# Conv operands from chunks held in SBUF, second product pairs, prepared conv-output weights and moved places in a one-core hybrid decoder layer

## The chip, the cores and the metric

One core of a Trainium2 chip runs the whole layer. The metric is device time in microseconds (us), the median of the timed runs, lower is better. The engines are named as the profile names them: PE (matrix products), PEld (its weight loads), DVE (vector), ACT (scalar, activations and casts), POOL (GpSimd) and SP, which computes nothing and issues DMAs. Each engine takes its instructions in the order in which they stand in its own queue, so an instruction that waits holds everything behind it on that engine; a DMA issue that waits on SP or POOL holds the later issues of that queue.

## The reference

The input `x` has 2048 tokens of width 1024, float32, one layer:

```python
h = rms_norm(x, norm_g)
u = jnp.einsum('bsd,dc->bsc', h, w_in)
v_c, b_c, c_c, z_c, q, k, v, z_a, gate_logits = jnp.split(u, SPLIT_POINTS, axis=-1)
y_c = b_c * causal_depthwise_conv(c_c * v_c, conv_w)      # width 3
y_c = y_c * jax.nn.silu(z_c)
y_a = jnp.einsum('bsc,cd->bsd', y_c, w_conv_out)
q = rms_norm(q.reshape(b, s, N_Q_HEADS, HEAD_DIM), q_norm_g)    # 16 heads of 64
k = rms_norm(k.reshape(b, s, N_KV_HEADS, HEAD_DIM), k_norm_g)   # 4 heads
o = sliding_window_attention(q, k, v, sinks) * jax.nn.silu(z_a)  # window 128, sink per head
y_b = jnp.einsum('bsc,cd->bsd', o, w_attn_out)
g_a, g_b = jnp.split(jax.nn.sigmoid(gate_logits + gate_b), N_BRANCHES, axis=-1)
return x + jnp.einsum('bsd,de->bse', g_a * y_a + g_b * y_b, w_out)
```

## The kernel before

**Tiles and units.** The tokens are worked on in two tiles `t` of 1024. Everything is kept transposed, features on the partitions. A *unit* produces 256 output features for the 1024 tokens of a tile, as a 2x2 problem (two halves of 128 features, two halves of 512 tokens) with seven instead of eight products; a product is 12 matmuls of 128x512 (4 chunk pairs, and three float32r terms: high x high, high x low, low x high) in `product` (L674). The names in the profile follow: `X`, `V`, `Y` are the PSUM banks of a unit, `w..._ah/_al`, `_sh/_sl`, `_th/_tl`, `_d` its weights for products 1 and 2, 5 and 6, 3 and 7, and 4, each as a high and a low part, and `oph`, `ophc`, `ophy`, `ophwo` are the seven forms of the right-hand operand (the normalised input, the gated attention output, the gated conv output, the output weights). Forms 5, 6, 7 and 4 are made of sums and differences of raw chunks on DVE; every form is then split by `op_split` (L339): a cast on ACT for the high part and a subtraction on DVE for the low part. There are 28 buffers for forms.

`sunit` runs one unit, seven products, with some banks' values passed through the one bank `Y`. `spair` runs two units side by side, product by product (1, 1, 2, 2, 5, 5, ...), with its own banks for the second.

**Weights.** `plan` lists the units; `piece`, called once a tick, casts and splits the next weights into a ring of 8 buffers (`wpool`). For the first two units of `yb` (the attention output projection) the high and low weights of all products are made once, in tile 0 (`prepare`), written to DRAM (`wpd`) and fetched in both tiles (kind `"L"` of the plan, L516).

**What sets the order.** A *tick* is one product of PE. `put(n, f)` places a piece of work at tick `n`, and `run` emits, after each product, what stands at that tick. So the tables of numbers at the head of the file fix the order on ACT, DVE, POOL and SP; the hardware waits come from buffers and semaphores alone. Buffers are given out in rotation: `big` (19 of 128x512), `upool` (2 of 128x1026), so a tile may have to wait until the last reader of a much earlier one is done.

**The places that matter here**, in order of time:

- The next tile's statistics (`next_stats`, L1883 and L849): eight blocks of `x` are loaded into `upool` and squared on ACT at the ticks `STAT_AT`.
- Attention: 32 blocks per tile, each a row of steps at fixed distances from its tick in `STEPS_0/1`; the step with the products `po` (L1371) comes 13 ticks after the scores. Its operands go through ACT (`xh`, `yp`), DVE (`xl`) and four selections on POOL (L1354).
- `z` and `za` units (the two SiLU gates), while in tile 0 `prepare` makes the `yb` weights and the next tile is normalised, and in tile 1 `wo_sums` reads the output weights into `upool`, and writes four differences per chunk pair to DRAM (`wsd`).
- Keys of tile 1 (`fin_k`): their inverse root mean squares are turned into rows, written to DRAM (`krd`), read back spread over 64 partitions (`krb`, L1185), and DVE multiplies the keys by them (`scaled`). `K_AT` has the distances: sums, spread (2 ticks between two of four), scaled.
- The end of tile 1: `yb` of tile 1 (4 units: one pair, two single), `ya` (the conv output projection) of tile 0 and of tile 1 (4 units each: one pair, two single), then the output projection. A `ya` result is multiplied by its gate `th` (loaded from `gd` into `upool`, L1505) and added to `mt` in DRAM by a DMA of POOL with accumulation (L1520).
- The operand of `ya`: the gated conv output lies in DRAM (`ocd`). `csum` loads its chunks on SP (`cr`), makes the four sums on DVE and writes them to DRAM (`csd`); `conv_op` loads each of the 28 forms' source, a raw chunk or a sum, on POOL (`oc`) and splits it.

Of the kernel before, what the change touches and what calls it, by code (L numbers as in the profile page):

```python
# [15 lines left out]
P = 128  # L16
# [42 lines left out]
K_AT = (1, 0, 2)  # L59
V_TURN = 2  # L60
# [15 lines left out]
CSUM_0 = (2, 14, 11, 20)  # L76
CSUM_1 = (54, 66, 67, 76)
CONV_0 = (2, 3, 1, 3, 0, 7, 2, 8, 4, 0, 7, 6, 4, 11, 11, 1, 1, 8, 11, 12, 12, 16, 13, 16, 16, 12, 8, 15)
CONV_1 = (5, 0, 0, 2, 1, 2, 0, 6, 8, 5, 7, 9, 5, 11, 11, 0, 8, 8, 11, 10, 16, 15, 14, 16, 16, 11, 12, 13)
# [8 lines left out]
ROOTS_AT = (-39, -37, -17, -8)  # L88
NX_LOAD0 = (10, 9, 8, 11, 12, 8, 13, 12)
NX_LOAD1 = (15, 15, 15, 14, 18, 17, 17, 20)  # L90
NX_1 = (16, 16, 19, 18)
NX_2 = (19, 19, 22, 27)
NX_SUM5 = (20, 17, 20, 21)
NX_5 = (21, 17, 21, 22)
NX_SUM6 = (22, 22, 23, 25)
NX_6 = (24, 26, 26, 29)
NX_SUM7 = (22, 18, 21, 23)
NX_3 = (20, 29, 27, 26)
NX_SUM4 = (25, 29, 29, 33)
NX_7 = (25, 19, 29, 34)  # L100
NX_4 = (36, 30, 29, 36)
# [24 lines left out]
CA0_4 = (16, 15, 16, 16)  # L126
CA1_4 = (17, 17, 18, 18)
CA0_FIRST = (3, 3, 5, 10)
CA1_FIRST = (1, 4, 4, 10)
CA0_SECOND = (9, 9, 7, 12)  # L130
CA1_SECOND = (5, 6, 9, 11)
CA0_THIRD = (14, 13, 15, 11)
CA1_THIRD = (14, 13, 14, 11)
CA0_LAST = (13, 13, 11, 15)
CA1_LAST = (16, 14, 14, 15)
# [19 lines left out]
def block_kernel(  # L155
# [59 lines left out]
    csd = [dram.tile([4, KP, P, H], F32, name=f"csd{t}") for t in range(NT)]  # L215
# [411 lines left out]
    def piece():  # L627

        if not todo and (len(ready) > used[0] or not open_prep()):
            return None  # L630
        n, i, cost, last, f = todo[0]
        if tick[0] < held.get(n, 0):
            return None
        need = [2 * n + i] if plan[n][0] == "P" else [2 * n, 2 * n + 1][: 1 + min(i, 1)]
        if live[0] + cost > WRING or any(k not in raws for k in need):
            return None
        todo.pop(0)
        live[0] += cost
        rawlive[0] -= last
        return f()  # L640
# [495 lines left out]
    def fin_k(t):  # L1136
# [3 lines left out]
        def fin(i, q, val):  # L1140
# [20 lines left out]

            put(tick[0] + K_AT[0], sums)

# [7 lines left out]
        def turned(r):  # L1171
# [435 lines left out]
    for t in range(NT):  # L1607
# [244 lines left out]
    def attention(t, places):  # L1852
        for r, n in enumerate(places):
# [17 lines left out]
            put(n + O_, step("o", lambda g, j=j, b=b: att_values(t, j, b, g["w"], g["v"])))  # L1871
            put(n + O_ + 1, step("z", lambda g, j=j, b=b: att_out(t, j, b, g["o"])))
            put(n + S_, step("t", lambda g, j=j, b=b: att_sum(t, j, b, g["z"])))
# [73 lines left out]
    conv = [{} for _ in range(NT)]  # L1947

    def csum(t, n, j):
        raw, to = {}, csd[t]  # L1950

        def ld():
            for i in range(2):
                for q in range(2):
                    o = raw[i, q] = slot([P, H], F32, f"cr{t}_{j}_{i}_{q}")
                    nc.sync.dma_start(o, ocd[t][2 * j + i, :, hs(q)])

        def out(m, a, b, c):
            sub(a, b, c)
            nc.sync.dma_start(to[m, j], a)  # L1960

        put(n, ld)
        put(n + 2, lambda: out(0, raw[0, 0], raw[0, 1], raw[0, 0]))
        put(n + 3, lambda: out(1, raw[0, 1], raw[1, 1], raw[0, 1]))
        put(n + 4, lambda: out(2, raw[1, 1], raw[1, 1], raw[0, 0]))
        put(n + 5, lambda: out(3, raw[1, 0], raw[1, 0], raw[1, 1]))

    def conv_op(t, n, m, j):
        src = {8: (0, 1), 1: (0, 0), 2: (1, 0), 3: (1, 1)}.get(m)
        got = slot([P, H], F32, f"oc{t}_{m}_{j}")  # L1970
        if src:
            nc.gpsimd.dma_start(got, ocd[t][2 * j + src[0], :, hs(src[1])])  # L1972
        else:
            nc.gpsimd.dma_start(got, csd[t][(5, 7, 6, 4).index(m), j])
        put(n, lambda: op_split(f"y{t}", m, j, got, conv[t]))

    tick0 = 0
    for t in range(NT):
# [7 lines left out]

        attention(t, [t0 + n for n in (STEPS_0, STEPS_1)[t]])
# [143 lines left out]
```

## Time and profile before

| | |
|---|---|
| median of 3 runs | 1920.59 us (1916.62 to 1921.56) |
| the profiled execution, its own time | 1915.99 us |
| its span in the trace | 1914.3 us |
| PE busy | 1884.9 us (98%), 8622 matmuls |
| DVE / ACT / POOL busy | 1578.9 / 1004.1 / 606.1 us (82 / 52 / 32%) |
| DMA | 422.14 MB, mean 221 GB/s |
| tile 0: keys, values to `za` / `yb` | 0 to 731 us / 731 to 810 us |
| tile 1: keys, values to `za` / `yb` | 810 to 1523 us / 1523 to 1599 us |
| `ya` of both tiles / output projection | 1599 to 1756 us / 1756 to 1914 us |

PE is busy nearly throughout, so its rows are read for what is missing: where a matmul starts late, the trace gives the idle time before it and the engine whose semaphore ended it. A wait row reads "who waited <- for what: total us, times, longest us". SPq rows are DMA issues; the time beside them is that of issuing.

### The profile page before, as it was taken

Reading aid. Unit: us, or ns where it says so; the run is one execution under the profiler, and the core shown is the slowest. Engines: PE = TensorE matmul, PEld = TensorE weight load, DVE = VectorE, ACT = ScalarE, POOL = GpSimd, SP = SyncE. Lnnn points to the kernel's source line nnn. Section 1 sums busy time; section 2 is a strip of 40 time slices with the busy share of each in tenths; the row PEclk is TensorE's granted clock in tenths of the full one; section 3 lists DMA queues with packets and bytes.
Section 4 is the critical chain, followed back from the end, with each engine's and each line's share of the span. In section 5 each row is a group of like instructions: output and inputs, shape, how many; then the busy total and the mean of one; then the engine's idle time right before and its main releaser. Section 6 shows DMA issues by size and latency. Waiting matters only on the chain.

```text
span 1914.3 us, 27564 instructions
## 1 busy us (share of the span) xinstructions
PE 1884.9 (98%) x8622; PEld 1564.2 (82%) x8622; DVE 1578.9 (82%) x2643; ACT 1004.1 (52%) x1995; POOL 606.1 (32%) x874
## 2 busy tenths in 40 slices
PE   9999999999999999998999999999999999999999
PEld 7888888888887887887888888888878888778787
DVE  7988898798888878978988889888878779687654
ACT  7665455556666444455545555666643435344321
POOL 2073334335655000026424344454620012331000
PEclk9999999999999999999999999999999999999999
DMA  8286556668787789638655555787889679998653
GB/s 295 79 236 175 168 169 179 213 205 250 234 245 237 262 295 307 230 111 227 163 163 158 161 161 186 237 245 227 254 282 324 236 273 330 298 250 245 226 175 110
DMA packets 230817, 422.14 MB, mean 221 GB/s; under 512 B 30928, under 2 KB 105680, under 8 KB 220688
## 3 DMA queue, kind: packets, MB, share of 16 engines
q1 hardware_dynamic: 195456, 329.88, 52.7%
q0 software_dynamic: 32768, 86.28, 16.7%
q10 hardware_dynamic: 2448, 4.23, 0.7%
q8 instruction: 69, 1.13, 0.2%
q14 instruction: 76, 0.62, 0.1%
HBM read 282.63 MB, written 137.64 MB: 220 GB/s over the span
## 4 chain that ended last, share of the span: by engine, by line
PE 76%; DVE 7%; DMA 7%; issue 5%; ACT 3%; POOL 2%; SPq 1%; DVEq 0%; ACTq 0%; POOLq 0%
PE Y L674 29%; PE Xcv L674 3%; PE Vcv L674 3%; PE Xza L674 2%; PE Vza L674 2%; PE Vyb L674 2%; PE Xgb L674 2%; PE Vgb L674 2%; PE Xyb L674 2%; PE po L1371 2%; PE Vga L674 2%; PE Xga L674 2%; PE Vo L674 2%; PE Vb L674 2%; PE Xb L674 2%
## 5 line engine op out<-in xcount | busy, mean ns | idle before, releaser
L1333 POOL DMA_DIRECT2D x<-fd x256 | 139.9, 552 | 126.0 <-DMA fd<-f 55.7
L1306 ACT ACTIVATE p<-s,st,rq 128x128 f32<-128x128 f32 x256 | 113.0, 450 | 0.2 <-issue 0.2
L1354 POOL TENSOR_SCALAR_AFFINE_SELECT xh<-xh 64x512 fp32r<-64x512 f32 x64 | 59.8, 934 | 160.3 <-DVE xl L308 87.4
L1326 POOL DMA_DIRECT2D fd<-f x64 | 36.7, 573 | 215.5 <-DVE f L308 186.0
L1210 POOL DMA_DIRECT2D vd<-v x16 | 9.9, 622 | 220.1 <-DVE v L308 219.9
L674 PE MATMUL Xcv<-oph,wcv_ah 128*128 128x512 f32 x256 | 79.0, 390 | 0.0
L1354 POOL TENSOR_SCALAR_AFFINE_SELECT xl<-xl 64x512 fp32r<-64x512 f32 x64 | 65.7, 1027 | 4.4
L1520 POOL DMA_DIRECT2D mt<-th x32 | 27.8, 868 | 121.7 <-DVE th L308 117.7
L1972 POOL DMA_DIRECT2D oc<-ocd x24 | 14.6, 654 | 146.1 <-ACT ophc L339 119.5
L1354 POOL TENSOR_SCALAR_AFFINE_SELECT yp<-xl 64x512 fp32r<-64x512 f32 x64 | 58.5, 915 | 3.1
L1354 POOL TENSOR_SCALAR_AFFINE_SELECT yp<-yp 64x512 fp32r<-64x512 f32 x64 | 57.5, 898 | 4.2
L308 DVE SCALAR_TENSOR_TENSOR y<-u,cols,y 128x512 f32<-128x512 f32 x64 | 53.3, 833 | 3.8 <-ACT y L1420 2.7
L674 PEld LDWEIGHTS Xcv<-oph,wcv_ah 128*128 128x128 f32 x256 | 47.6, 188 | 9.6
L308 DVE TENSOR_TENSOR o<-po,o 64x256 f32<-64x256 f32 x128 | 53.4, 417 | 1.0
L308 DVE TENSOR_TENSOR p<-p,st 128x512 f32<-128x512 f32 x64 | 50.4, 787 | 3.7 <-DVE st L308 0.4
L1109 POOL DMA_DIRECT2D q2d<-q_h x64 | 44.2, 691 | 25.9 <-ACT q_h L1104 14.8
L495 ACT CAST wcv_sh<-wcv_raw 128x1024 fp32r<-128x1024 f32 x16 | 16.8, 1052 | 67.8 <-DVE wcv_raw L308 67.7
L1306 ACT ACTIVATION_READ_ACCUMULATOR p<-s,st,rq 128x1 f32 x256 | 50.5, 197 | 0.0
L674 PE MATMUL Xcv<-oph,wcv_al 128*128 128x512 f32 x128 | 49.8, 389 | 0.0
L674 PE MATMUL Y<-oph,wcv_d 128*128 128x512 f32 x192 | 46.9, 393 | 1.7 <-DVE vr L308 1.5
L1383 ACT COPY o<-po 64x256 f32<-64x256 f32 x128 | 47.1, 368 | 2.3
L1109 POOL DMA_DIRECT2D q2d<-q_l x64 | 44.1, 689 | 13.0 <-DVE q_l L308 5.2
(691 smaller groups left out, 6557.2 us busy)
## 6 DMA issues: line engine op xcount, KB each, us to landing
gd<-th SPq DMA_DIRECT2D x64, 256.0 KB, 2.7
wcv_raw<-in_w_units SPq DMA_DIRECT2D x16, 1024.0 KB, 5.5
q<-q2d SPq DMA_DIRECT2D x64, 256.0 KB, 5.5
v<-vd SPq DMA_DIRECT2D x128, 128.0 KB, 3.5
fd<-f POOLq DMA_DIRECT2D x64, 256.0 KB, 4.1
x<-fd POOLq DMA_DIRECT2D x256, 64.0 KB, 3.2
th<-gd SPq DMA_DIRECT2D x64, 256.0 KB, 5.2
x<-in_x SPq DMA_DIRECT2D x16, 512.0 KB, 6.4
```

The source lines that it names most:

```text
L308: r = f(*args, **kw)
L495: return (lambda: nc.scalar.copy(hi, src), lambda: vec.tensor_tensor(out=lo, in0=src, in1=hi.bitcast(F32), op=ALU.subtract))
L674: nc.tensor.matmul(ps, lhsT=w[:, j, :], rhs=b[:, m, :], start=start and j == 0 and i == 0, stop=j == KP - 1 and i == 2, skip_group_check=n ...
L1109: nc.gpsimd.dma_start(q2d[t][j][half, q * 2 * HB : (q + 1) * 2 * HB, i, e, :], src[HALVES[e]].bitcast(F32).rearrange("p (b x) -> p b x", x ...
L1306: nc.scalar.activation(out=p[:, i, :], in_=sg[:, i, HD : 3 * HD], func=AF.Exp, bias=st[:, 1, i : i + 1], scale=rv[:, i // 2, i % 2 : i % 2 ...
L1326: nc.gpsimd.dma_start(fd, f)
L1333: nc.gpsimd.dma_start(x[QUADS[k]], src[k])
L1354: nc.gpsimd.affine_select(out=d4, in_=s4, pattern=[[0, 2], [-32 * sg, 2], [0, G], [-sg, 32]], compare_op=ALU.is_gt if prev else ALU.is_ge, ...
L1371: nc.tensor.matmul(po[:, cs], lhsT=v2[:, kind, :], rhs=xx[:, :, h * HD : (h + 1) * HD], start=n == 0, stop=n == 2)
L1383: nc.scalar.copy(ov, pov[oth, :, e])
L1520: nc.gpsimd.dma_start(to, m, accum_op=ALU.add)
L1972: nc.gpsimd.dma_start(got, ocd[t][2 * j + src[0], :, hs(src[1])])
```

## The change

1. **Conv operand.** `csum`, `conv_op` and the DRAM tensor `csd` go. The 16 raw chunks of a tile are loaded once each, on POOL, into `big` buffers, and the sums are made in place, as the forms of the next tile's input already are (`first_sum`, `second_sum`, `third`, `last_sum`, `form`).
2. **Pairs.** In tile 1 the third and fourth `yb` units become a pair; so do the third and fourth `ya` units of tile 0. For `ya` of tile 1 they stay single.
3. **`ya` weights.** Those of the first two `ya` units are made by `prepare` in tile 1's `z`/`za` units, written to DRAM and fetched for both tiles. Two prepared pieces may be fetched in one tick.
4. **`wo_sums`** moves from tile 1's `z`/`za` units to the last gate units (two of four) and the last `za` units.
5. **Keys.** The four spreads and multiplications get ticks of their own, the value turns come one tick later.
6. **Places.** `STAT_AT` goes from 3 to 7 ticks apart; three attention blocks of tile 0 (10, 11 and 30) get their `po` products and what follows one tick later; `HOLD`, `PREP_*`, `NX_*`, `CA*`, `WO_FORM_AT` get new numbers.

```diff
-K_AT = (1, 0, 2)
-V_TURN = 2
+K_SUMS_AT = 1
+K_SPREAD = (1, 1, 5, 7)
+K_SCALED = (5, 7, 9, 11)
+V_TURN = 3
...
-CSUM_0 = (2, 14, 11, 20)
-CSUM_1 = (54, 66, 67, 76)
...
-WO_SUMS_AT = (1, 9, 18, 27)
...
+CO0_LOAD0 = (-5, -5, -9, -7, -4, -3, -3, 4)
...
+CO1_LOAD0 = (-7, -3, -2, -2, -3, -4, -3, -1)
...
+WO_SUMS_AT = (160, 169, 219, 227)
 WO_AHEAD = 3
-THS_AT = (9, 8)
-YB_PAIRS = (2, 1)
-HOLD = (9, 11, 7, 11, 9, 8, 9)
-STAT_AT = (105, 112, 116, 119, 121, 122, 125, 128)
+THS_AT = (8, 6)
+YB_PAIRS = (2, 2)
+YA_PAIRS = (2, 1)
+HOLD = (7, 11, 7, 9, 8, 7, 8, 10, 5)
+STAT_AT = (112, 119, 126, 133, 140, 147, 154, 161)
...
+VALUES_LATER = ((0, 10), (0, 11), (0, 30))
...
+PREP_E = (9, 12, 16, 16, 18, 23, 25, 30, 33, 33)
+PREP_F = (17, 25, 24, 19, 29, 32, 40, 35, 37, 35)
...
-    def piece():
+    def piece(more=True):
...
-        return f()
+        got = f()
+        if more and plan[n][0] == "L" and todo and plan[todo[0][0]][0] == "L":
+            piece(False)
+        return got
...
-                put(tick[0] + K_AT[1] + 2 * n, lambda i=i, q=q: spread(i, q))
-                put(tick[0] + K_AT[2] + 2 * n, lambda i=i, q=q: scaled(i, q))
+                put(tick[0] + K_SPREAD[n], lambda i=i, q=q: spread(i, q))
+                put(tick[0] + K_SCALED[n], lambda i=i, q=q: scaled(i, q))
...
-            paired.add(len(plan))
             for j in range(NJ):
+                if j in (0, 2)[: YA_PAIRS[i]]:
+                    paired.add(len(plan))
                 at_(("ya", i, j))
+                if j < 2:
+                    plan[-1] = ("L",) + plan[-1][1:]
...
-            put(n + O_, step("o", lambda g, j=j, b=b: att_values(t, j, b, g["w"], g["v"])))
+            late = int((t, r) in VALUES_LATER)
+            put(n + late + O_, step("o", lambda g, j=j, b=b: att_values(t, j, b, g["w"], g["v"])))
...
-    def csum(t, n, j):
...
-    def conv_op(t, n, m, j):
...
+    conv = [{"raw": {}, "ops": {}} for _ in range(NT)]
+
+    def conv_ops(t, n1):
+        st = conv[t]
+
+        def ld(c, q):
+            h = st["raw"][c, q] = slot([P, H], F32, f"oc{t}_{c}_{q}")
+            nc.gpsimd.dma_start(h, ocd[t][c, :, hs(q)])
+
+        for q, ns in enumerate(((CO0_LOAD0, CO1_LOAD0)[t], (CO0_LOAD1, CO1_LOAD1)[t])):
+            for c, n in enumerate(ns):
+                put(n1 + n, lambda c=c, q=q: ld(c, q))
...
+        for j in range(KP):
+            put(n1 + (CO0_SUM5, CO1_SUM5)[t][j], lambda j=j: first_sum(j, st))
+            put(n1 + (CO0_5, CO1_5)[t][j], lambda j=j: form(f"y{t}", 5, j, st))
...
+        if t + 1 == NT:
+            for j in range(KP):
+                wo_sums(t0 + WO_SUMS_AT[j], j)
...
-        if t == 0:
-            for j in range(2):
-                prepare(("yb", j), tick[0], (PREP_A, PREP_B)[j])
+        for j in range(2):
+            prepare((("yb", "ya")[t], j), tick[0], (PREP_A, PREP_B, PREP_E, PREP_F)[2 * t + j])
...
-                rest += y_units(i, 0, conv[i], 1)
+                conv_ops(i, n0 + 7 * (NJ * i + NJ - 2))
+                rest += y_units(i, 0, conv[i]["ops"], YA_PAIRS[i])
```

Three places where the tables move instructions. The rows are the program's order on one engine, with no time in them; line numbers of the changed kernel are larger by about 30.

ACT in tile 0, around the last conv unit and the unit `b_3`: `ACTIVATE x_` is the square of a loaded block of `x`, `COPY Y` the copy for which PE's next product waits, `CAST wb_3_..` the weights of the unit. Before:

```order
L849 ACTIVATE x_4_3779,ss_651<-x_4_3779 128x1024
L495 CAST wb_3_ah<-wb_3_raw 128x1024
L1383 COPY o_1_2_3863<-po_1_2_3821 64x4x2x32 x2
L1340 CAST xh_1_3_3866<-x_1_3_3702 128x512
L1341 CAST yp_1_3_3868<-x_1_3_3702 64x512
L849 ACTIVATE x_5_3798,ss_651<-x_5_3798 128x1024
L1402 COPY u_7_3781<-Xcv_7_3782 128x512
L495 CAST wb_3_d<-wb_3_raw 128x512
L495 CAST wb_3_sh<-wb_3_raw 128x1024
L849 ACTIVATE x_6_3898,ss_651<-x_6_3898 128x1024
```

and in the change:

```order
L522 CAST wb_3_ah<-wb_3_raw 128x1024
L1370 CAST xh_1_3_3850<-x_1_3_3694 128x512
L1371 CAST yp_1_3_3852<-x_1_3_3694 64x512
L1432 COPY u_7_3771<-Xcv_7_3772 128x512
L522 CAST wb_3_d<-wb_3_raw 128x512
L1413 COPY o_1_2_3873<-po_1_2_3843 64x4x2x32 x2
L522 CAST wb_3_sh<-wb_3_raw 128x1024
L522 CAST wb_3_th<-wb_3_raw 128x1024
L1370 CAST xh_1_4_3946<-x_1_4_3812 128x512
L1371 CAST yp_1_4_3948<-x_1_4_3812 64x512
L879 ACTIVATE x_2_3907,ss_649<-x_2_3907 128x1024
L722 COPY Y<-Xb_3_3966 128x512
```

Three squares stood among the ten rows; now there is one, ahead of the copy of `Y`, and the copy `o_1_2` of a block with later `po` now follows `wb_3_d`.

DVE in tile 1, the second and third query units: `k_.._t<-k_.._t,krb` are the key multiplications, `k_.._l` the low parts after a cast of ACT, `Vq` and `q_.._t` the sums for which PE waits. Before:

```order
L308 SCALAR_TENSOR_TENSOR q_0_1_0_l<-q_0_1_0_t,gqk,q_0_1_0_h 128x512
L308 TENSOR_TENSOR k_0_0_t<-k_0_0_t,krb_0_0_8660 128x512
L308 TENSOR_TENSOR wq_1_tl<-wq_1_raw,wq_1_th 128x1024
L308 STREAM_TRANSPOSE ptq_0_0_0_8717<-q_0_0_0_t 128x512
L308 TENSOR_TENSOR k_0_0_l<-k_0_0_t,k_0_0_h 128x512
L308 TENSOR_TENSOR k_0_0_t<-k_0_0_t,krb_0_1_8697 128x512
L308 STREAM_TRANSPOSE ptq_0_1_1_8747<-q_0_1_1_t 128x512
L308 TENSOR_REDUCE qss_0_8492<-ptq_0_0_0_8717 128x16
L308 TENSOR_TENSOR Vq_1_8728<-s5q_1_8741,Y 128x512
```

and in the change:

```order
L335 SCALAR_TENSOR_TENSOR q_0_1_0_l<-q_0_1_0_t,gqk,q_0_1_0_h 128x512
L335 TENSOR_TENSOR wq_1_tl<-wq_1_raw,wq_1_th 128x1024
L335 STREAM_TRANSPOSE ptq_0_0_0_8714<-q_0_0_0_t 128x512
L335 TENSOR_TENSOR k_0_0_t<-k_0_0_t,krb_0_0_8628 128x512
L335 STREAM_TRANSPOSE ptq_0_1_1_8736<-q_0_1_1_t 128x512
L335 TENSOR_REDUCE qss_0_8475<-ptq_0_0_0_8714 128x16
L335 TENSOR_TENSOR Vq_1_8717<-s5q_1_8730,Y 128x512
```

The first key multiplication now stands behind two instructions that do not need it, and of the other key work ahead of `Vq` nothing is left.

SP at the change from `yb` to `ya` of tile 0: `wya_.._ah/_al/_sh/_sl` are the fetched weights, `th_0_0<-gd` the first gate of the pair (into one of the two `upool` buffers), `mt<-th` results of the last `yb` units. Before, the weights came raw, 1 MB each, among the loads and stores of the sums; in the change:

```order
L1548 DMA mt_114<-th_2_1_15551 128x512 x2
L543 DMA wya_0_ah<-wpd_ya_0_13816 128x1024
L543 DMA wya_0_al<-wpd_ya_0_13816 128x1024
L1548 DMA mt_114<-th_2_2_15652 128x512
L1535 DMA th_0_0_15786<-gd_0_115 128x512 x2
L1548 DMA mt_114<-th_2_2_15652 128x512
L543 DMA wya_1_ah<-wpd_ya_0_13820 128x1024
L543 DMA wya_1_al<-wpd_ya_0_13820 128x1024
L1548 DMA mt_114<-th_2_3_15678 128x512
L543 DMA wya_0_sh<-wpd_ya_1_13817 128x1024
L543 DMA wya_0_sl<-wpd_ya_1_13817 128x1024
```

The second unit's first weights stand behind the load of `th_0_0`, which needs a buffer that the stores of `th_2_1` release. At the start of `ya` of tile 1 the order is the same, but there the buffer is released by POOL's accumulating DMAs.

More of the change, by code (lines that the diff above doesn't have):

```diff
@@ new lines @@
+CO0_SUM5 = (5, 4, 3, 6)
+CO0_SUM6 = (9, 10, 13, 14)
+CO0_SUM7 = (5, 6, 12, 12)
+CO0_SUM4 = (14, 15, 16, 21)
+CO0_1 = (0, 3, 3, 5)
+CO0_2 = (5, 6, 10, 16)
+CO0_5 = (8, 6, 5, 14)
+CO0_6 = (10, 12, 15, 19)
+CO0_3 = (8, 17, 13, 8)
+CO0_7 = (7, 8, 12, 21)
+CO0_4 = (23, 17, 16, 25)
+CO1_LOAD0 = (-7, -3, -2, -2, -3, -4, -3, -1)
+CO1_LOAD1 = (-7, -4, -2, 0, 3, 0, 0, 0)
+CO1_SUM5 = (4, 3, 5, 6)
+CO1_SUM6 = (9, 6, 12, 14)
+CO1_SUM7 = (5, 8, 8, 12)
+CO1_SUM4 = (12, 15, 14, 22)
+CO1_1 = (2, 3, 3, 2)
+CO1_2 = (5, 6, 8, 13)
@@ L1160, in reduce @@
                     put(tick[0] + 1, rms)
-            put(tick[0] + K_AT[0], sums)
+            put(tick[0] + K_SUMS_AT, sums)
         left = [4]
@@ L2019, in block_kernel @@
             next_tile(t + 1, tick[0] + 7 * 2 * NJ)
-        if t + 1 == NT:
-            for j in range(KP):
-                wo_sums(tick[0] + WO_SUMS_AT[j], j)
-        if t == 0:
-            for j in range(2):
-                prepare(("yb", j), tick[0], (PREP_A, PREP_B)[j])
+        for j in range(2):
+            prepare((("yb", "ya")[t], j), tick[0], (PREP_A, PREP_B, PREP_E, PREP_F)[2 * t + j])
         for n, (key, j, fin, _) in enumerate(zs):
-            if n == NJ - 1 and t + 1 == NT:
-                for i in range(NT):
-                    for j in range(NJ):
-                        csum(i, tick[0] + (CSUM_0, CSUM_1)[i][j], j)
             if n + 1 < len(zs):
```

118 lines of the change are left out of this document (53 added, 65 removed).

## The prediction

> **What bounds the kernel now.** First the page's head and its engine row:
>
> ```profile
> span 1914.3 us, 27564 instructions
> PE 1884.9 (98%) x8622; PEld 1564.2 (82%) x8622; DVE 1578.9 (82%) x2643; ACT 1004.1 (52%) x1995; POOL 606.1 (32%) x874
> ```
>
> PE computes nearly all the time, and the change alters none of its matmuls. What can be won or lost is PE's idle time: 1914.3 - 1884.9 = 29.4 us, plus any time at a lower clock. So the second view is that of PE's waits, longest first, over the whole span:
>
> ```profile
> PE Y L674 <- ACT Y L692: 4.0, 3, 3.2
> PE Y L674 <- DVE q_t L308: 3.1, 1, 3.1
> PE Y L674 <- DVE s5ya L308: 2.7, 1, 2.7
> PE Y L674 <- DVE Vq L308: 2.1, 2, 1.5
> PE po L1371 <- POOL xl L1354: 1.8, 2, 1.4
> PE Y L674 <- DVE vr L308: 1.5, 2, 1.2
> ...
> PE po L1371 <- POOL yp L1354: 1.3, 1, 1.3
> ...
> PE Xyb L674 <- DMA wyb_ah<-wpd_yb: 1.0, 1, 1.0
> PE Xyb L674 <- DMA wyb_al<-wpd_yb: 0.9, 2, 0.5
> ...
> PE Y L674 <- DVE Vya L308: 0.6, 1, 0.6
> ```
>
> There is no standing bottleneck behind PE, only some ten separate stalls of 1 to 3 us, each with its own cause a step or two further back. I followed each back in the timelines of ACT, DVE and POOL, and count them one by one. The sum is made against the profiled execution, 1915.99 us; the median of the runs shown, 1920.59, lies 4.6 us above it, and I add that at the end.
>
> **Term 1, the statistics (`STAT_AT`).**
>
> ```profile
> 361.56 1.06 ACT L849 ACTIVATE x<-x 128x1024 f32<-128x1024 f32 x1 [3.78 <-DMA x<-in_x]
> 380.95 1.06 ACT L849 ACTIVATE x<-x 128x1024 f32<-128x1024 f32 x1 [3.82 <-DMA x<-in_x]
> SPq L1883 <- ACT x L849: 11.5, 4, 5.7
> 384.68 1.66 PE L674 MATMUL Y<-oph,wcv_d 128*128 128x512 f32 x6 [1.22 <-DVE vr L308]
> ```
>
> The loads of `x` wait on SP for a buffer that ACT's squares release (11.5 us in four waits), so twice the square waits 3.8 us for its load, and ACT's casts behind it are late. That delays `wb_d`, then `vr` on DVE, then PE (1.22), and in the same stretch the POOL selections of `po` (the 1.4 of the `xl` row). With 7 ticks between two blocks, no load meets an unread buffer. Gain 1.4 + 1.2 = 2.6 at most. The squares now stand directly ahead of a copy of `Y` eight times, two ticks after their load; a load that is late by a microsecond there costs part of that. I take -2.4; bounds -2.6 and +0.5.
>
> **Term 2, three later `po` (`VALUES_LATER`).** Block 30 is the stall in `z`:
>
> ```profile
> 615.67 0.38 PE L1371 MATMUL po<-yp,v 128*128 128x256 f32 x1 [1.31 <-POOL yp L1354]
> 616.50 0.38 PE L1371 MATMUL po<-xl,v 128*128 128x256 f32 x1 [0.44 <-POOL xl L1354]
> 617.28 1.05 PE L674 MATMUL Y<-oph,wz_sh 128*128 128x512 f32 x2
> ...
> 620.48 0.40 PE L674 MATMUL Y<-oph,wz_sl 128*128 128x512 f32 x1
> 620.71 0.62 PE L674 MATMUL Y<-oph,wz_sh 128*128 128x512 f32 x2
> 615.00:620.00 5.00, 3.89 (x12) 3.11 (x13) 3.19 (x6) 3.70 (x7) 1.37 (x2) 0.68 1.06 345
> 890.00:895.00 5.00, 3.70 (x16) 3.06 (x17) 4.93 (x9) 3.04 (x6) 4.39 (x7) 1.00 0.91 239
> ```
>
> POOL is late by 1.31 + 0.44. The granted clock in these 5 us is 0.68 (the column before the DMA share), and the eight matmuls from 617.28 to 620.48 take 3.20 us, where at 0.23 apiece (the last step) they would take 1.84: another 1.36. The later tick, at least one product, covers the delay, so gain 1.31 + 0.44 + 1.36 = 3.1. A loss of clock does not follow every stall: at 890 to 895, with 3.07 us idle (the row at 891.30 below), the clock stayed 1.00, so I price none for new stalls. Bounds -3.1 and 0 (the delay repeats a tick later). I take -3.1. What is late next is that block's output, which no unit reads until `za`.
>
> The Trainium skill, TensorE: Matmul & The Clock Gate (What's actually happening), says that the clock falls to half after an idle window of about 3.4 us in a window that runs freely. By that rule the 1.75 us here would not lower it and the 3.07 us at 891 might; the trace shows the opposite of both. If it held for stalls above 3.4 us, the four stalls of the slower rival below would cost some 1.4 more each, 1936 for 1931.
>
> **Term 3, the key roots.**
>
> ```profile
> 875.71 0.69 DVE L308 TENSOR_TENSOR k_t<-k_t,krb 128x512 f32<-128x512 f32 x1 [3.39 <-DMA krb<-krd]
> 879.35 0.69 DVE L308 TENSOR_TENSOR k_l<-k_t,k_h 128x512 fp32r<-128x512 f32 x1 [1.17 <-ACT k_h L339]
> 884.24 0.69 DVE L308 TENSOR_TENSOR k_l<-k_t,k_h 128x512 fp32r<-128x512 f32 x1 [1.18 <-ACT k_h L339]
> 888.15 0.69 DVE L308 TENSOR_TENSOR k_t<-k_t,krb 128x512 f32<-128x512 f32 x1 [0.82 <-DMA krb<-krd]
> 891.30 1.89 PE L674 MATMUL Y<-oph,wq_d 128*128 128x512 f32 x7 [3.07 <-DVE q_t L308]
> ```
>
> DVE loses 3.39 + 1.17 + 1.18 + 0.82 = 6.6 us in waits of the key work, and `Vq` and `q_t` behind it are late: PE waits 2.1 + 3.1 = 5.2. In the new order two instructions (a low part and a transpose) move ahead of the first multiplication, and each `k_l` gets other work between itself and its cast. The first DMA wait will not go entirely: the two instructions fill about 1.9 of 3.39. With some 5 of 6.6 us recovered on DVE, both PE stalls nearly vanish; the 0.6 that the second `Vq` wait adds (2.1 - 1.5) may stay, as two multiplications move into that unit. I take -4.5; bounds -5.2 and -2. `kd` comes three ticks later, some 20 ticks ahead of the first attention load.
>
> **Term 4, `wo_sums` out of `z`, `prepare` into it.**
>
> ```profile
> 1390.24 0.60 ACT L1477 ACTIVATE zs<-Y 128x512 f32<-128x512 f32 x1 [6.92 <-DMA ocd<-zin]
> 1367.85 1.60 SPq L1576 DMA_DIRECT2D wos<-in_w_out  x2
> SPq L1469 <- DMA od<-o: 6.8, 1, 6.8
> ```
>
> PE's 3.2 on `ACT Y` is the end of this chain: SP waits 6.8 us for a buffer that `od<-o` still reads, `ocd<-zin` behind it goes late, and ACT waits for the buffer that this frees. The 1 MB of `wos` in front of `od<-o` made it slow. It leaves; but nine ticks into `z` 1 MB of `wp_ya` stands in the same position ahead of another `od<-o` and `zin`. So the stall can come back one unit later. I take -3.2 + 2.0 = -1.2; bounds -3.2 and +1.5. `prepare` itself adds 14 casts on ACT and 22 subtractions and sums on DVE, of 0.6 to 0.7 us each (the ACT row here, the DVE rows of term 3); they lie in the idle time of both engines in `za`, and where that is gone each costs PE its length.
>
> **Term 5, `csum` gone.**
>
> ```profile
> 1644.47 0.69 DVE L308 TENSOR_TENSOR cr<-cr,cr 128x512 f32<-128x512 f32 x1 [5.37 <-DMA cr<-ocd]
> 1672.95 1.04 ACT L495 CAST wya_ah<-wya_raw 128x1024 fp32r<-128x1024 f32 x1 [6.22 <-DMA wya_raw<-in_w_units]
> 1600.00:1740.00 140.00, 136.49 (x599) 111.74 (x598) 110.40 (x159) 58.26 (x86) 42.23 (x61) 1.00 0.97 281
> ```
>
> The two stalls of `ya` (0.6 on `Vya`, 2.7 on `s5ya`) come from DVE waiting for a sum's chunks and from a raw weight that lands late in a stage with a DMA share of 0.97. PE's idle time there is 140 - 136.49 = 3.5. The new order has no `cr` load, and that unit is in a pair. I take -3.5; bounds -3.5 and 0.
>
> **Term 6, raw chunks and second pairs.** Sixteen chunks sit in 19 rotating buffers, and the forms are made from them during the second `yb` pair and the second `ya` pair of tile 0. The nearest row is the second `yb` pair of tile 0 with the next tile's forms, built alike:
>
> ```profile
> 780.00:835.00 55.00, 54.41 (x239) 43.89 (x239) 53.05 (x82) 30.18 (x51) 2.47 (x4) 1.00 0.38 124
> ```
>
> PE idles 0.59 there. Two such places give +1.2. The DMA share there is only 0.38, so the upper bound is +4; the lower 0.
>
> **Term 7, fetched `ya` weights.** Two new starts with weights that need ring buffers of the pair before:
>
> ```profile
> wyb_al<-wpd_yb SPq DMA_DIRECT2D x2, 512.0 KB, 8.1
> 1522.71 10.90 PE Xyb L674 x48
> SPq L1505 <- DMA mt<-th: 55.2, 14, 9.9
> mt<-th POOLq DMA_DIRECT2D x28, 256.0 KB, 5.8
> ```
>
> At tile 0's `yb` the fetch took 8.1 us to land and PE waited 1.9; at tile 1's (1522.71) it waited 0. A product takes 10.90/4 = 2.7 us, and in a pair the second unit's first weights find a free buffer only when product 7 is done, three to four products (8 to 11 us) ahead of use. They also stand behind the load of a gate `th`, which waits for `mt<-th` to land, up to 9.9 us. So +2 at each start, +4 in all; bounds 0 and +10. In bytes little changes: at 256 KB a transfer the 64 of `csum` (16 MB), 24 of 56 `oc` (6) and four raw weights (4) go, two raw loads and 28 stores of `prepare` (9) and 56 halves of fetches (14) come, 3 MB net of some 420.
>
> The Trainium skill, DMA: Bandwidth & Descriptors (Issuing engines are not separate DMA queues), says that DMAs from all engines share the same 16 DMA engines. By it, chunk loads on POOL don't relieve the fetches on SP, which land as slowly as at 0.97; that would put term 7 near +5 rather than +4.
>
> **Sum.** -2.4 - 3.1 - 4.5 - 1.2 - 3.5 + 1.2 + 4 = -9.5: 1906.5 for a profiled execution, 1911.1 for a median. `HOLD`, `NX_*`, `CA*`, `WO_FORM_AT` and the startup I leave at nothing.
>
> **The rivals.**
>
> *All gains, no new stalls:* terms 1 to 5 at their best, 6 and 7 at 0: -2.6 - 3.1 - 5.2 - 3.2 - 3.5 = -17.6, median 1903. For it: tile 1's `yb` start without a stall. Against: PE would then idle about 13 us in the whole span.
>
> *The end gives it back:* terms 1 to 3 hold (-10), term 4 returns in full (0), and fetches and chunks cost +10 against -3.5. About -3.5, median 1917, within 0.3%. It is also what remains if the moved ticks don't remove the waits they aim at.
>
> *Slower, by SP's queue in `ya`:* the second unit's first and third weights, in both fetched `ya` pairs, stand behind a `th` load. If each of these four issues waits the 9.9 us seen, less than the lead of 8 to 11 us is left for a landing of 8.1, and PE waits 5 to 8 at each, 20 to 32 in all; with the other terms at -13.5 that is +6.5 to +18.5, median about 1931. It decides from a mean wait of 3.4 us at each of the four. For it: the 55.2 us of such waits, and POOL's queue, where chunk loads that wait for buffers stand ahead of `mt<-th`. Against: tile 1's `yb`, with stores of SP in POOL's place, shows none.
>
> **How the numbers follow.** Forecast 0.42, all gains 0.20, given back 0.18, slower 0.20. A measurement of this kernel can tell about 0.3% (5.8 us) from no change, so faster 0.62, same 0.18, slower 0.20. The likeliest case alone spans 1906 to 1916 (term 7 from 0 to +9); the range 1899 to 1930 reaches into both outer cases.
>
> **What would show it.** Right: no `x<-in_x` wait on ACT between 340 and 400; `po` at 615 without idle time and clock 1.00; DVE's `krb` wait under 2 us; PE waits of 1 to 3 us for `wya_ah`/`wya_al` at the two pair starts. Wrong: a PE wait on `wya_th` or `wya_tl`, or on `ophy` behind an `oc` load, above 3 us; ACT's `zs` again behind `ocd<-zin`; or a new wait of the gate units behind the squares.

## The result, and the profile after

The changed kernel takes 1915.55 us (median of 20 executions, 1912.27 to 1927.6), the kernel before 1919.22 us on the same chip (median of 20, 1916.35 to 1925.25): a ratio of 0.9982, with 95% between 0.9971 and 0.9993. A second set of runs gave 0.9979 (0.9970 to 0.9988). So the change gains 3.5 to 4 us where 9.5 were forecast, a fifth of a per cent: real, but under the 0.3% that the prediction drew as the line to "no change". In the table further down, an effect "against the change" is the difference to the mean of these two ratios, 0.99805, times 1919 us; each such difference is uncertain by some 3 us, one against the kernel before by some 2.

The first profile of the change comes from its slowest execution, 1927.6 us, so a second profile was taken as well, of an execution of 1913.3 us (span 1911.6). The page's head and the engine row of the first profile:

```profile
span 1925.8 us, 27444 instructions
PE 1894.3 (98%) x8622; PEld 1569.9 (82%) x8622; DVE 1568.2 (81%) x2633; ACT 996.2 (52%) x1993; POOL 593.4 (31%) x850
```

PE's idle time is 31.5 us where it was 29.4, and PE's busy time rose by 9.4 us although it computes the same 8622 matmuls: most of that is a lower clock. The view of PE's waits (engine, line, what it waited for: us in total, times, longest), same profile:

```profile
PE Y L704 <- ACT Y L722: 7.0, 5, 3.4
PE Y L704 <- DVE Vq L335: 3.2, 1, 3.2
PE Xya L704 <- DMA wya_ah<-wpd_ya: 3.0, 1, 3.0
PE Y L704 <- DVE zs L335: 2.0, 1, 2.0
...
PE Vya L704 <- DMA wya_th<-wpd_ya: 1.9, 1, 1.9
...
PE Vya L704 <- DMA wya_tl<-wpd_ya: 0.9, 2, 0.6
...
PE Xya L704 <- DMA wya_al<-wpd_ya: 0.7, 2, 0.5
PE Y L704 <- DVE q_t L335: 0.6, 1, 0.6
```

Of the rows shown of before, `s5ya` is gone, `vr` is down to 0.3, the longest of `po` fell from 1.4 to 0.7 and `q_t` from 3.1 to 0.6. `Vq` rose from 1.5 to 3.2 at its longest and `zs` from 0.6 to 2.0. New are the four rows of fetched `ya` weights (6.5 us), and a longest wait on `ACT Y` that now lies in the gate stage, at 459. So many of the stalls moved rather than vanished. What `ya` costs shows in how many matmuls run between 1600 and 1740 us, the number in brackets behind PE's busy time. Before it was 599 (the row stands in the prediction). The change, first profile:

```profile
1600.00:1740.00 140.00, 133.14 (x555) 107.23 (x554) 83.52 (x126) 41.40 (x68) 29.59 (x40) 0.95 0.87 246
```

and the second profile of the change:

```profile
1600.00:1740.00 140.00, 133.68 (x572) 108.61 (x571) 87.33 (x129) 43.20 (x69) 32.99 (x44) 0.98 0.88 248
```

At 0.227 us a matmul, 44 and 27 fewer are 10.0 and 6.1 us lost in a stage where the prediction's terms 5 to 7 come to +1.7. The DMA share there fell from 0.97 to 0.87, which speaks against a want of DMA engines as the cause of the late weights. SP's timeline of the change (start, length, line, transfer), first profile, shows what they wait for:

```profile
1611.00 0.32 SPq L543 DMA_DIRECT2D wya_th<-wpd_ya  x1
1611.41 1.40 SPq L543 DMA_DIRECT2D wya_tl<-wpd_ya  x1
1621.50 0.80 SPq L1535 DMA_DIRECT2D th<-gd  x2
1622.40 0.38 SPq L543 DMA_DIRECT2D wya_th<-wpd_ya  x1
...
1672.14 0.56 SPq L543 DMA_DIRECT2D wya_ah<-wpd_ya  x1
1672.80 0.39 SPq L543 DMA_DIRECT2D wya_al<-wpd_ya  x1
1684.01 0.85 SPq L1535 DMA_DIRECT2D th<-gd  x2
1684.96 0.38 SPq L543 DMA_DIRECT2D wya_ah<-wpd_ya  x1
```

Between 1612.8 and 1621.5, and between 1673.2 and 1684.0, SP issues nothing: it stands at a `th` load whose buffer an accumulate `mt<-th` still reads. The second unit's weights are issued right behind, and land too late. PE's timeline behind the first of the two (the bracket is the idle time before the row and its releaser):

```profile
1629.41 0.70 PE L704 MATMUL Vya<-ophy,wya_th 128*128 128x512 f32 x2 [1.87 <-DMA wya_th<-wpd_ya]
1630.69 0.79 PE L704 MATMUL Vya<-ophy,wya_tl 128*128 128x512 f32 x1 [0.58 <-DMA wya_tl<-wpd_ya]
1631.29 1.05 PE L704 MATMUL Vya<-ophy,wya_th 128*128 128x512 f32 x2
1632.14 0.63 PE L704 MATMUL Vya<-ophy,wya_tl 128*128 128x512 f32 x1
1632.57 1.05 PE L704 MATMUL Vya<-ophy,wya_th 128*128 128x512 f32 x2
```

Three matmuls take 1.28 us here (1631.29 to 1632.57), 0.427 apiece where 0.227 is usual, and the granted clock between 1630 and 1635 is 0.50. It stays so until 1636.4.

### The profile page after: what moved, and what is told of

Same layout as the page of the kernel before. It is cut to its first block, busy times and chain, and to the rows that moved or that the text cites. A ratio compares the mean times of both kernels' runs of the same rounds, so it can differ in the third digit from the quotient of the medians.

```text
span 1925.8 us, 27444 instructions
## 1 busy us (share of the span) xinstructions
PE 1894.3 (98%) x8622; PEld 1569.9 (82%) x8622; DVE 1568.2 (81%) x2633; ACT 996.2 (52%) x1993; POOL 593.4 (31%) x850
## 4 chain that ended last, share of the span: by engine, by line
PE 74%; DMA 9%; DVE 7%; issue 5%; ACT 2%; POOL 1%; SPq 1%; DVEq 0%; POOLq 0%; ACTq 0%
PE Y L704 29%; PE Vcv L704 4%; PE Xcv L704 4%; PE Xza L704 2%; PE Vo L704 2%; PE Xo L704 2%; PE Vza L704 2%; PE Vga L704 2%; PE Xgb L704 2%; PE Vb L704 2%; PE Xga L704 2%; PE po L1401 2%; PE Vq L704 2%; PE Xb L704 2%; PE Vgb L704 2%
## 5 line engine op out<-in xcount | busy, mean ns | idle before, releaser
L1988 POOL DMA_DIRECT2D oc<-ocd x32 | 19.7, 673 | 138.7 <-DMA wyb_al<-wpd_yb 116.5
L335 DVE TENSOR_TENSOR ophy<-oc,ophy 128x512 fp32r<-128x512 f32 x56 | 36.8, 685 | 23.6 <-ACT ophy L366 23.6
L366 ACT CAST ophy<-oc 128x512 fp32r<-128x512 f32 x56 | 31.8, 619 | 33.1 <-DVE oc L335 23.8
```

Of the source, the lines that this page charges most:

```text
L335: r = f(*args, **kw)
L366: nc.scalar.copy(hi, src)
L1988: nc.gpsimd.dma_start(h, ocd[t][c, :, hs(q)])
```

## The experiments

Twelve kernels ran, the change itself once more among them, each in 5 to 12 executions beside the kernel before. First the measured effects in one table.

| run | edit | ratio to before (95%) | effect, us |
|---|---|---|---|
| the change again | none | 0.9979 (0.9970 to 0.9988) | -4.0 against before |
| e1 | `th` loads of `ya` later | 0.9942 (0.9928 to 0.9956) | -7.4 against the change |
| e2 | `STAT_AT` undone | 0.9985 (0.9973 to 0.9997) | +0.9 against the change |
| e3 | `STAT_AT`, `VALUES_LATER`, keys undone | 1.0009 (0.9998 to 1.0021) | +1.7 against before, +5.5 against the change |
| e4 | squares two ticks later | 0.9960 (0.9945 to 0.9974) | -3.9 against the change |
| e5 | e1 and e4 | 0.9933 (0.9919 to 0.9948) | -9.1 against the change |
| e6 | keys undone | 1.0005 (0.9993 to 1.0018) | +4.7 against the change |
| e7 | e5, key products a tick later | 0.9938 (0.9919 to 0.9957) | -8.2 against the change |
| e8 | before with `wo_sums` moved alone | 0.9996 (0.9987 to 1.0005) | -0.8 against before |
| e9 | `VALUES_LATER` undone | 1.0010 (0.9995 to 1.0025) | +5.7 against the change |
| e10 | `ya` weights from raw loads | 0.9981 (0.9967 to 0.9995) | +0.1 against the change |
| e12 | before with the `th` loads later | 0.9986 (0.9976 to 0.9995) | -2.7 against before |

**e1, the `th` loads of `ya` behind the weights.** In the change, with the third and fourth load of a pair at ticks 8 and 9, and the next unit's first two ticks later:

```diff
-  ((0, 0), (1, 1), (outs[0][0] + 1, 2), (THS_AT[t], 3)), outs[1][0] + 1))
+  ((0, 0), (1, 1), (outs[0][0] + 1, 2), (THS_AT[t], 3)) if w
+      else ((0, 0), (1, 1), (8, 2), (9, 3)), outs[1][0] + (1 if w else 3)))
```

> The changed kernel, with the third and fourth load of th in each pair of ya, and the first for the next unit, issued some ticks later, so that on SP they stand behind the weights of the second unit and not ahead. Theory A (SP's order): in the changed kernel's profile SP waits 8.6 us (1612.9 to 1621.5) and 10.7 us (to 1684.0) at a th load for mt<-th, and wya_th and wya_ah, wya_al issued behind it are late; PE's stalls of 2.0, 0.8, 3.1 and 0.9 us for these weights (6.8 us) fall under 1 us together and the low clock behind them goes too (some 3 us more), so about 7 to 10 us faster than the changed kernel. Theory B (the fetches are late because their buffers come free late and the DMA engines are busy): the weights' issues move forward by little, the stalls stay within 1 us of 6.8, and the time stays within 2 us.

Measured: 1908.03 us, 7.4 less than the change. SP's timeline of e1:

```profile
1602.91 0.32 SPq L543 DMA_DIRECT2D wya_th<-wpd_ya  x1
1603.33 0.38 SPq L543 DMA_DIRECT2D wya_tl<-wpd_ya  x1
1605.66 0.32 SPq L543 DMA_DIRECT2D wya_th<-wpd_ya  x1
1606.07 0.38 SPq L543 DMA_DIRECT2D wya_tl<-wpd_ya  x1
1614.97 0.92 SPq L1535 DMA_DIRECT2D th<-gd  x2
```

SP still waits (1606.5 to 1615.0), but now the second unit's `wya_th` goes out 2.8 us behind the first's instead of 11.4. In the same stretch of e1:

```profile
1600.00:1740.00 140.00, 138.35 (x609) 113.93 (x608) 92.24 (x137) 47.74 (x76) 32.99 (x44) 1.00 0.93 265
```

609 matmuls instead of 555 and 572, at clock 1.00. Theory A holds; the DMA engines move more in the same time (265 GB/s for 246), so theory B falls. What stays of the fetches is PE waits of 0.5, 0.5 and 1.3 us, 2.3 together: more than the 1 us that theory A expected, and less than the +4 that the prediction gave them.

**e12, the same edit in the kernel before.**

> The kernel before with the th loads of the ya pairs later, and nothing else. The prediction's fifth term took the late raw weight and the late chunks of a sum in ya (PE's stalls of 0.6 and 2.7 us) to come from csum's transfers at a DMA share of 0.97: then 0 to 1 us, with the stalls still there. Theory A' (there too SP stood still: its th loads wait up to 9.9 us for mt<-th, with cr<-ocd and the raw weight issued right behind): 3 to 5 us faster than the kernel before, so that csum itself cost little.

Measured: 2.7 us faster than the kernel before, with `csum` still in place. In the first of these two fences is e12's stretch of `ya`, in the second its one wait of PE there:

```profile
1600.00:1740.00 140.00, 138.68 (x609) 113.69 (x609) 112.72 (x163) 59.04 (x88) 42.17 (x61) 1.00 0.98 287
```

```profile
PE Y L674 <- DVE s5ya L308: 1.3, 1, 1.3
```

The stalls of 0.6 and 2.7 us shrink to 1.3, and the matmuls rise from 599 to 609, at a DMA share of 0.98. So in the kernel before, too, most of the loss in `ya` came from the standing `th` loads, with `cr<-ocd` and the raw weight behind them, not from the amount that `csum` moved. The gain is just short of the 3 to 5 that were expected.

**e10, `ya` weights from raw loads.** No `prepare` for `ya` and no fetched halves; `HOLD` as the raw pairs had it.

```diff
-        for j in range(2):
+        for j in range(2 if t == 0 else 0):
             prepare((("yb", "ya")[t], j)
...
                 at_(("ya", i, j))
-                if j < 2:
+                if j < 0:
                     plan[-1] = ("L",) + plan[-1][1:]
...
-HOLD = (7, 11, 7, 9, 8, 7, 8, 10, 5)
+HOLD = (7, 11, 7, 9, 8, 9, 8, 8, 5)
```

> The changed kernel with the weights of the two first ya pairs formed from raw loads as before (no fetched halves of ya, none prepared in the stage of z). The prediction's seventh term: 4 us faster than the changed kernel. Theory A (behind SP's order the fetches cost 10): 7 to 10 us faster, as with the th loads moved. Rival (the conversions of four more raw units cost DVE and ACT in ya what the fetches cost SP): within 2 us of the changed kernel, with PE's waits for weights behind DVE in their place.

Measured: no difference. The waits of PE in `ya` are of other kinds, in e10's profile:

```profile
PE Xya L704 <- DVE ophy L335: 4.8, 1, 4.8
PE Vya L704 <- DVE wya_sl L335: 1.4, 1, 1.4
```

DVE's timeline ahead of the first of them has the form (`ophy`) behind four sums of raw weights and a low part, without a gap:

```profile
1610.61 2.74 DVE L335 TENSOR_TENSOR wya_raw<-wya_raw 128x512 f32<-128x512 f32 x4
1613.27 1.22 DVE L335 TENSOR_TENSOR wya_sl<-wya_raw,wya_sh 128x1024 fp32r<-128x1024 f32 x1
1614.40 0.68 DVE L335 TENSOR_TENSOR ophy<-oc,ophy 128x512 fp32r<-128x512 f32 x1
```

The rival holds: formed from raw loads, the pairs cost DVE about what the fetches cost through SP's order. e1 lies 7.5 us below e10, but e10 has the early `th` loads; raw weights with the late ones were not run, so it isn't shown that fetched weights are the better kind.

**e2 and e4, the statistics.** In e2 `STAT_AT` has its old ticks:

```diff
-STAT_AT = (112, 119, 126, 133, 140, 147, 154, 161)
+STAT_AT = (105, 112, 116, 119, 121, 122, 125, 128)
```

In e4 each square stands four ticks behind its load:

```diff
-            put(n0 + n + 2, lambda b=b: square(b))
+            put(n0 + n + 4, lambda b=b: square(b))
```

> The changed kernel with the loads of x for the next tile's statistics at their old ticks. The prediction's first term (the new places gain 2.4): about 2.4 us slower than the changed kernel. Theory A (in the gate stage the square in front of the copy of Y waits 6.3 us for its load, which SP issues behind attention's loads, and PE's stalls of 3.6 and 1.3 us, with two of 0.6, cost more than the 2.6 removed, before any loss of clock): 3 to 5 us faster than the changed kernel, with PE's waits for Y between 455 and 510 under 1 us in all.

> The changed kernel with each of the eight squares four ticks behind its load of x instead of two, so that it no longer stands in front of the copy of Y. Theory A (what costs is that the copy of Y stands behind a square that waits for its load): PE's stalls of 3.6, 1.3, 0.6 and 0.6 us on ACT's Y in the gate stage fall under 1 us together, and the time falls by 4 to 6 us with the low clock behind the first. Rival (ACT has no room for a square anywhere in the gate stage, the wait or its 1.1 us only meets the next conversion): 0 to 2 us, with new waits of PE for weights or for po.

ACT's timeline of the change (first profile) shows what the new places cost:

```profile
457.91 1.06 ACT L879 ACTIVATE x<-x 128x1024 f32<-128x1024 f32 x1 [6.32 <-DMA x<-in_x]
458.88 0.19 ACT L879 ACTIVATION_READ_ACCUMULATOR x<-x 128x1 f32 x1
458.97 0.58 ACT L722 COPY Y<-Xga 128x512 f32<-128x512 f32 x1
```

The square waits 6.3 us for its block, the copy of `Y` stands behind it, and PE waits 3.4. With the old places (e2) PE waits elsewhere:

```profile
PE Y L704 <- DVE vr L335: 3.4, 2, 3.0
```

So the term as it stands is worth 0.9 us, neither the 2.4 of the prediction nor a loss of 3 to 5. In e4 the whole rest of `ACT Y` is:

```profile
PE Y L704 <- ACT Y L722: 1.5, 2, 1.3
```

and the longest of it lies at 1382, in `z`, not in the gate stage. The gain of 3.9 us is just short of the 4 to 6 that were expected, within its uncertainty. Against the old places the later squares gain 3.9 + 0.9 = 4.8 us: the new places are worth at least the prediction's 2.4, and the wait in front of the copy ate most of it.

**e3, e6 and e9, parts of the first tile undone.** e3 undoes the three edits of terms 1 to 3, e6 the key roots, e9 the later `po`:

```diff
-VALUES_LATER = ((0, 10), (0, 11), (0, 30))
+VALUES_LATER = ()
```

```diff
-K_SPREAD = (1, 1, 5, 7)
-K_SCALED = (5, 7, 9, 11)
-V_TURN = 3
+K_SPREAD = (0, 2, 4, 6)
+K_SCALED = (2, 4, 6, 8)
+V_TURN = 2
```

> The changed kernel with the statistics, the three later po and the key roots at their old places: only the part behind them (wo_sums, prepare, the raw chunks, the second pairs and the fetched ya weights) is new. The prediction (terms 4 to 7: -1.2 - 3.5 + 1.2 + 4): 0.5 us slower than the kernel before, so about 4 us slower than the changed one. Theory A (the first three terms held at about -10 and the end costs 6 to 7): 6 to 7 us slower than the kernel before. Theory C (the first three terms gained little, since their stalls came back elsewhere, and the end is about even): 0 to 1 us faster than the kernel before, 2 to 4 slower than the changed one.

> The changed kernel with the key roots' old places. The prediction's third term: 4.5 us slower than the changed kernel. Theory D (DVE is full in the queries' stage, 9.6 of 10 us from 880 on, so that the key work only moves PE's wait from q_t, 3.1, to Vq of the next unit, 3.1): within 1.5 us of the changed kernel, with the old two stalls of about 1.4 and 3.3 us in place of 0.7 and 3.3.

> The changed kernel without the three later po. The prediction's second term: 3.1 us slower than the changed kernel, with PE's stalls of 1.3 and 0.5 us at 615 back. Rival (the gain is given back 11 us later, where PE waits 1.1 to 2.2 us for wz_d behind DVE's zs in all profiles of the change, and not before it): within 1 us of the changed kernel.

e6 lost 4.7 us, close to the prediction's term and against theory D; its waits at that place are these two:

```profile
PE Y L704 <- DVE q_t L335: 3.4, 1, 3.4
...
PE Y L704 <- DVE Vq L335: 1.6, 1, 1.6
```

They are 5.0 us for 3.8 in the change (0.6 and 3.2), so the visible waits explain 1.2 us of the 4.7 and theory D had the picture right; the rest is within the uncertainty or in the clock behind the second long stall, and stays open. e9 lost 5.7, with these rows back:

```profile
PE po L1401 <- POOL yp L1384: 2.1, 2, 1.3
...
PE po L1401 <- POOL xl L1384: 1.4, 3, 0.5
```

The prediction's 3.1 lies inside that. Its rival, that `zs` at 627 gives the gain back, falls. e3 puts the three terms together at 5.5 us, less than the 11.3 that e2, e6 and e9 add up to. With some 3 us on each, the runs don't say how much of this is an interaction.

**e8, `wo_sums` alone.** In the kernel before, `wo_sums` is issued at the change's ticks, and nothing else is changed:

```diff
-WO_SUMS_AT = (1, 9, 18, 27)
+WO_SUMS_AT = (160, 169, 219, 227)
...
+        if t + 1 == NT:
+            for j in range(KP):
+                wo_sums(t0 + WO_SUMS_AT[j], j)
         attention(t, [t0 + n for n in (STEPS_0, STEPS_1)[t]])
...
-        if t + 1 == NT:
-            for j in range(KP):
-                wo_sums(tick[0] + WO_SUMS_AT[j], j)
```

> The kernel before with one part of the change alone: the sums for wo moved out of the stage of z, to the new ticks in the attention and z stages; no prepare for ya. The prediction's fourth term at its best: SP no longer holds od<-o back, ACT's zs don't wait 6.9 us for ocd<-zin, and PE's 3.2 us on ACT's Y go: 3.2 us faster than the kernel before, a little more if the clock falls behind that stall. Rival: the sums cost the same where they go, since POOL's selections for po are late there (0.6 and 0.7 us, at 1343 in the runs of the change) and the gain is under 1.5 us.

Measured: 0.8 us, the rival's side. ACT waits 5.8 us for `ocd<-zin` instead of 6.9, and SP for `od<-o`:

```profile
SPq L1469 <- DMA od<-o: 5.1, 1, 5.1
```

5.1 instead of 6.8: without the 1 MB of `wos` in front of it `od<-o` is still slow. PE's wait on ACT's `Y` there falls from 3.2 to 2.4 only, and 50 us earlier, where the sums went, PE waits for `po` as the rival said, with no such wait in the profile of before:

```profile
PE po L1371 <- POOL yp L1354: 1.0, 1, 1.0
PE po L1371 <- POOL xl L1354: 0.6, 2, 0.4
```

In the change SP's wait is 3.6 (first profile), and PE's wait on ACT's `Y` there 1.6; in the second profile PE's is gone. What else shortened it was not tried.

**e5 and e7, putting edits together.** e5 has the edits of e1 and e4; e7 has besides

```diff
-K_SCALED = (5, 7, 9, 11)
+K_SCALED = (6, 8, 10, 12)
```

> The changed kernel with both edits of the runs before: the th loads of ya later, and the squares four ticks behind their loads. The two stages lie 1100 us apart, so if each edit removes its own wait the gains add: 0.40 and 0.22 per cent, 11.8 us less than the changed kernel, ratio to the kernel before near 0.992. If both only shifted where PE's clock falls, they would not add: 8 us or less.

> Both edits (th loads of ya later, squares four ticks behind their loads) and the four multiplications of the key roots one tick later each. In the profiles of the changed kernel DVE waits 2.0 us for the first krb and twice 1.2 us for a cast of k_h, and the fourth multiplication stands in front of Vq, for which PE then waits 3.2 us. A tick later the first wait falls under other work and the fourth multiplication stands behind Vq: PE's wait under 1 us, 2 to 4 us faster than with both edits alone. Rival (DVE is full from 880 to 940, so that any order leaves PE 3 us in front of some step of the queries): within 1 us.

e5 reaches 1908.28 us, 0.9933: 9.1 less than the change, where the two effects add to 11.3 and 8 would have meant no addition. In its profile ACT waits at another place of the gate stage, 6.3 us for a store `od<-o` at 490, so part of the square's gain can return behind the same queue. e7 is no different (0.9938): its profile has

```profile
PE Y L704 <- DVE Vq L335: 3.0, 1, 3.0
```

as in the change (3.2 and 3.1), and DVE still waits three times 1.2 us for the cast of `k_h`. The rival holds. e5 beats both kernels, 0.67% under the kernel before; it can't be told from e1 alone (0.9942).

**The change again.**

> The changed kernel itself once more, for a second profile: the first came from an execution of 1927.6 us, 12 above the median. If the stalls in the gate stage (3.6 us) and in ya (6.8 us) are the kernel's own, this profile has them within 2 us; what lies between the executions is then the low clock behind them (about 12 us of PE time in matmuls at half speed in the first profile). If the stalls are fewer, the spread is in the landing times.

The second profile (1911.6 us) has the stall for `Vq` (3.1) and 4.4 us of waits at the second pair start again, 1.5 at the first pair, but 1.7 instead of 3.4 at a gate unit and less than half of the time at half clock. Both were at work: the landing times vary, and the clock behind the stalls. For the clock, the fourteen profiles together (from 100 us on) list every gap by which one matmul's start to the next exceeds 0.227 us, and whether at least four matmuls at half pace come within 5 us behind it:

```
excess, us     gaps   followed by half pace
0.4 to 0.8      137      7
0.8 to 1.2       30      7
1.2 to 1.6       38      8
1.6 to 2.2       13      3
2.2 to 2.9       10      8
over 2.9         25     21
```

(A short gap next to a long one counts in its own row.) Behind 29 of 35 gaps over 2.2 us some seven matmuls run at 0.427 us instead of 0.227: another 1.5 us each time.

## Why the prediction was wrong

**The step that failed is term 7, and its size.** "So +2 at each start, +4 in all; bounds 0 and +10." It measured about +10: e1 takes 7.4 us away by SP's order alone and leaves 2.3, so 9.7 in place of 4. The rows agree: 6.5 us of waits for these weights and 4.6 us at half pace behind them in the first profile of the change, 5.9 and 2.2 in the second. Put into the sum, -9.5 + 5.7 = -3.8, against -3.5 and -4.0 measured; that it comes out so closely is luck, since two other misses cancel (last paragraph of this section). The mechanism was on the page of the prediction, as the third rival: `th` loads that wait for `mt<-th`, with the second unit's weights behind them. It decides, as written, "from a mean wait of 3.4 us at each of the four"; the change has waits of 8.7 and 10.8 us ahead of two of the four, and PE's stalls there are 2.5 and 3.5 us and not 5 to 8. It was kept at 0.20 because tile 1's `yb` start showed no stall "with stores of SP in POOL's place". That start was the wrong comparison: in `ya` the buffers come free by accumulates, and the row that spoke for the rival, 55.2 us of such waits, took in the very stage (between 1600 and 1740 alone the kernel before has 68.3, in 13 waits).

**The clock was priced at nothing** on the strength of the row at 890 to 895, 3.07 us idle at clock 1.00. Three gaps over 2.2 us of the one profile of before, all without a slow stretch behind them, are three of the six exceptions among 35. The prediction took a profile with luck for the rule; what the luck was, the last section shows. In the first profile of the change the 23 matmuls at half pace behind the two `ya` stalls are 4.6 us of the 10. The Trainium skill, TensorE: Matmul & The Clock Gate (What's actually happening), gives half clock after an idle window of about 3.4 us that runs freely. Half pace, the length and the free run agree (stretches of 3.41 us or twice that, last section); that gaps of 2.2 to 2.9 us bring it 8 times in 10 differs, and the measurement decides.

**Term 1** (-2.4): 0.9 us. Its wait went, and the sentence on squares "directly ahead of a copy of `Y`" named what took its place, at an upper bound of +0.5 in all. The loads there stand behind eight loads of attention on SP, 6.3 us were waited, and e4 shows that the place cost some 4. This is a second step that failed, and the prediction's own sign of being wrong, "a new wait of the gate units behind the squares", is what came.

**Terms 2 and 3** (-3.1, -4.5): right in sign, and in size within the uncertainty (-5.7 and -4.7 by themselves; together with term 1 only -5.5). For term 2 the sign held: no idle time at 615 and clock 1.00. For term 3 the view that "both PE stalls nearly vanish" was wrong: `q_t` fell from 3.1 to 0.6, but `Vq` rose from 1.5 to 3.2 at its longest, and e7's later multiplications left it at 3.0.

**Term 4** (-1.2): e8 measures 0.8 for the half that gains. The cause given, 1 MB of `wos` in front of `od<-o`, carries only 1.7 of the 6.8 us that SP waited.

**Term 5** (-3.5): the stalls went, but not for the reason given. The share of 0.97 was read as the limit; e12 gets 2.7 us with the transfers all there.

**Term 6** (+1.2): neither profile of the change shows a stall of PE for a form made from `oc` chunks above 0.3 us, so it held as far as it can be seen.

Between them the end (terms 4 to 7) was forecast at +0.5 and measured +1.7 in e3, and the first tile at -10 against -5.5. As e3 has term 7's 9.7 in its end, terms 4 to 6 must have gained some 8 and not 3.5; which of them was not tried, and each of these figures is uncertain by 2 to 3 us. So about 4.5 us too little in the first tile and as much too much in terms 4 to 6 cancel.

## What to carry to other kernels

When an in-order queue issues both loads that wait for a buffer and loads that a deadline hangs on, look at what stands behind each waiting issue in the order, not at how busy the DMA engines are: a few loads moved by three ticks or so were worth twice what the whole change gained. And price a new stall of more than about 2 us with the slow clock behind it, from several profiles; one profile can show none of it.

## What the runs showed of the hardware that was not expected

The clock falls behind stalls of 2 to 3 us, and not each time: 8 of 10 gaps of 2.2 to 2.9 us and 8 of 38 of 1.2 to 1.6 us were followed by a stretch at half pace, which starts up to some 3 us after the stall has ended. Equal stalls of one place behave differently from one execution to the next: the wait for `Vq`, 3.1 us long, had seven matmuls at half pace behind it in e1 and none in e4.

The clock that the profiles record shows what decides. Between 100 and 1900 us the fourteen profiles have 38 stretches at half clock, 31 of them 3.41 us long and 7 twice that, and within a profile their starts lie whole multiples of 3.413 us apart. So cut each profile into steps of 3.413 us on that grid. Of the steps at full clock in which PE idled for more than 55%, 30 of 31 were followed by half clock; between 45 and 55%, 8 of 16; below 45%, none of 7270. The stall for `Vq` on this grid, two steps of e1 and three of e4 (behind the comma PE's busy time, after POOL's the granted clock):

```profile
896.75:900.16 3.41, 0.98 (x4) 0.85 (x5) 2.93 (x5) 1.76 (x3) 1.06 (x2) 1.00 0.97 364
900.16:903.57 3.41, 3.41 (x9) 2.65 (x9) 3.19 (x6) 2.43 (x5) 2.52 (x5) 0.50 0.92 321
```

```profile
890.69:894.10 3.41, 1.69 (x8) 1.07 (x6) 2.11 (x8) 2.81 (x5) 2.16 (x4) 1.00 0.92 306
894.10:897.51 3.41, 2.05 (x9) 1.71 (x10) 3.41 (x6) 1.73 (x4) 1.64 (x4) 1.00 0.99 347
897.51:900.92 3.41, 3.41 (x17) 2.72 (x15) 3.19 (x6) 1.50 (x3) 3.14 (x6) 1.00 0.93 292
```

In e1 PE idles 71% of one step, in e4 the stall is cut in two, 50 and 40%. The three long stalls of the profile of before are each cut in the same way: 48 and 42% at 891, 50 and 42% at 1393, 50 and 29% at 1675. That was the prediction's luck. Against the start of the span the grid lies at another place in each of the fourteen profiles (from 0.03 to 0.95 of a step), so a stall of 2 to 3 us has a chance and not a price.

The clock is also a part of the spread of the change, 15 us between the fastest and the slowest of its 20 executions, whose mean clocks reach from 0.999 to 0.994 (time and clock correlate at -0.79); 8.0 us of the slowest are matmuls at half pace, 3.6 us of the second profile.
